# Gated conv blocks moved into the steps of the attention pipeline

## The chip, the cores and the metric

The kernel runs on one core of a Trainium2 chip. TensorE (PE) multiplies matrices, ScalarE (ACT) evaluates functions, VectorE (DVE) and GpSimd (POOL) work element by element, and SyncE (SP) starts the loads from DRAM. Each engine works through its own queue in order and waits where an operand is not ready. The metric is the device time of one execution in microseconds; less is better.

## The reference

Two layers of a diffusion backbone over 256 latent and 256 context tokens of width 1024, in float32. Each layer is a SwiGLU half step, a token mixing and a second SwiGLU half step. The change touches the mixing alone. It has three branches over the same normalised input, whose outputs are normalised, put side by side and projected (`merge_groups`):

```python
q_lat, kv_lat, k_pe, sg_in, cv_in = jnp.split(hn @ w_mix_in[l], splits, axis=-1)
q = mla_queries(q_lat, g_q_lat[l], w_q_up[l], g_q_head[l], rope)
k, v = mla_keys_values(kv_lat, k_pe, g_kv_lat[l], w_kv_up[l], g_k_head[l], rope)
attn = latent_attention(q, k, v, kc, vc)          # 8 heads, 96 wide keys, 64 wide values

def spatial_gating(sg_in, g_sgu, w_spatial, b_spatial):
    u, v = jnp.split(jax.nn.gelu(sg_in), 2, axis=-1)
    v = rms_norm(v.reshape(b, n, SG_GROUPS, SG_GROUP_DIM), g_sgu)
    ...
    return u * vs.reshape(b, n, SG_WIDTH)

def short_conv(cv_in, w_conv):
    b_gate, c_gate, xin = jnp.split(cv_in, 3, axis=-1)
    z = c_gate * xin
    y = lax.conv_general_dilated(z, ...)           # 3 taps, each channel by itself
    return b_gate * y
```

In the first layer (layer 0 below) latent and context tokens take all branches, 512 tokens. In the second (layer 1) the context gives keys and values only, so queries, gating and conv have 256 tokens.

## The kernel before

Weights come from DRAM in one stream, in the order of use. `Weights.pump` starts loads as room comes free and splits each weight in a high part (`whi`, ScalarE, L125) and a low part (`wlo`, L126, on GpSimd through the whole mixing, since `low` is "g" there). Each product is then three matmuls: high by high, high by low, low by high (`mm3`, L384 to L386, and `mm3x`, L389 to L391, with the operands' roles exchanged). At most five split weights are held. A weight `SPARE` in the stream is room lent to the attention. `W.hold` stops splitting except where `W.pump(n)` asks for it.

The schedule is written out by hand: jobs are emitted one after the other, and each engine's queue has its instructions in this order. PSUM has eight banks, six under the name `mm` and two under `sm`. A matmul into a bank waits until the bank's former readers are done.

The mixing of a layer (`mixing`, from L634) runs in this order:

- `kv_lat`, `kv_ctx`, `q_ctx` make key and query latents; `kv_tr` and `q_tr` transpose them (L720) and split them in two parts (L722, L723).
- `uv_lat` and `uv_ctx` project the gating's u and v; at their end `v_norm` normalises v for every tile of 128 tokens (L815 to L829: a square, a reduction, a root, four scalings, a split).
- `conv_block(0)` to `conv_block(3)`: 24 matmuls each. Of every three blocks the first gives the c gate, the second the product z and the three taps on VectorE (L872 to L877), the third the b gate's product (L879) and its squares.
- `spatial`: the gating's mixing over tokens, its product with u and its norm (L893 to L914).
- `conv_block(4)`, `conv_block(5)`, then `y_sg` (L921), which transposes the gating's result into the projection's input.
- `k_up` (L953): keys of four token tiles, each with a sum of squares, a root and an evacuation (L964 to L977). `y_cv_stats` takes the conv's norm, which is a root on ScalarE and a diagonal on VectorE.
- `q_up` (L1004): queries of each tile, whose rotary part is turned on GpSimd (L1037 to L1042).
- `y_cv`: the conv's norm is broadcast over TensorE and multiplied into the projection's input.
- `close_p1` gives the tiles of the first half back and opens those of the attention.
- `att(0)` to `att(11)`, the steps of a pipeline over heads. Step i takes `A(i)` (transposes of a head's queries and keys, L1076, each into an `sm` bank where there are four tiles), `B(i-2)` (scores, their maxima on VectorE, exponentials on ScalarE, the division by the sum on GpSimd, L1138), `C(i-3)` (transposes of the probabilities, L1158) and `Dv` (probabilities times values, L1181). The copies out of `A`'s banks (L1082 to L1087) are emitted in the step behind it; VectorE's share, `lows`, stands behind the maxima of `B`. Step 0 begins with `v_up`, the values of four tiles, whose evacuations are spread over steps 1 and 2. Steps 9 to 11 begin the output projection on the conv's and the gating's features.

In layer 0 `A` of a head fills both `sm` banks. ScalarE holds one set of functions at a time: `preload` puts a function of the next set ahead (Gelu before the u/v projection ends, Sqrt before `v_norm`, Exp at the end of `q_up`, Sqrt in step 10).

Of the kernel before, what the change touches and what calls it, by code (L numbers as in the profile page):

```python
# [39 lines left out]
# packed per-partition parameters: name -> columns for one layer  # L40
# [20 lines left out]
class Weights:  # L61
    """Streams weights in order: DRAM -> raw tile -> (high, low) float32r parts, ahead of their use.
    SPARE in the stream is room of one weight, left to other uses between its take and its done."""

    def __init__(self, nc, pool, raws):
# [18 lines left out]
        self.sub_fin = [False] * len(self.subs)  # L84
        self.sub_pref = 0
# [7 lines left out]
    def pump(self, preps=None):  # L93
        """Start the loads that have room, and prepare the parts (at most preps, when held back)."""
# [3 lines left out]
        while go:  # L98
# [8 lines left out]
            while left > 0 and self.prep_i < len(self.subs) and self.prep_i < self.sub_pref + SUBB:  # L107
# [67 lines left out]
def hybrid_trunk_kernel(ctx: ExitStack, tc: tile.TileContext, io: dict, out: bass.AP):  # L175
# [65 lines left out]
    # ---------------------------------------------------------------- weight specs  # L241
# [110 lines left out]
    def split_norm(src, dst_h, dst_l, rb, a, b=None, eng=None):  # L352
        """high and low parts of src * a * rb (+ b); returns the emission of the low part."""
# [17 lines left out]
    def staggered(makers):  # L371
        """runs emissions that return a follow-up, each follow-up one later"""
# [60 lines left out]
    # ---------------------------------------------------------------- FFN  # L433
    def ffn(l, which, ntok, tail, first=None):
        """tail(part): called by the last block to start the chain of what follows."""
# [28 lines left out]
        def first_two(W):  # L464
            """Blocks 0 and 1: the latent half while the norm of the context half is under way."""
# [147 lines left out]
    def boundary(l, i):  # L613
        """tail of the last block before norm i of layer l: work(0..2) is the ctx half in three parts."""
# [18 lines left out]
    # ---------------------------------------------------------------- mixing  # L633
    def mixing(l):  # L634
# [5 lines left out]
        def open_pools(W):  # L640
# [9 lines left out]
            st["row"] = per.tile([128, NROW], F32, name="row")  # L650
            SP.dma_start(out=st["row"], in_=io["row"][:, l])
            P["kvh"] = per.tile([128, 2, NTOK], F32R, name="kvh")
            P["kvl"] = per.tile([128, 2, NTOK], F32R, name="kvl")
# [9 lines left out]
            P["stok"] = P["guv"][:, :, 0:256]  # L663
            P["cvo"] = p1.tile([128, 2, NQ], F32, name="cvo")
# [948 lines left out]
```

## Time and profile before

| | |
|---|---|
| three runs, median | 1778.43 us (1777.52 to 1781.66) |
| the profiled execution, span | 1778.8 us |
| TensorE busy | 1715.4 us, 96% |
| VectorE, ScalarE, GpSimd busy | 1077.7, 661.1, 328.9 us |
| mean granted TensorE clock | 0.983 |

Times of the trace are microseconds from the start of the span. A matmul's recorded time is longer than the distance to the next one's start, since matmuls overlap in the array; the distance between starts is what a row of them costs. Square brackets behind an instruction give the idle time of its engine just before it and the instruction that ended the wait. `PEclk` is the granted clock of TensorE as a share of full speed.

### The profile page before, as it was taken

What the parts mean: (1) busy time and instruction counts of PE and PEld (TensorE: products, weight loads), DVE (VectorE), ACT (ScalarE), POOL (GpSimd) and SP (SyncE); (2) the same over time, 40 slices, a digit from 0 to 9 for tenths busy, and PEclk for the clock granted to TensorE, in tenths of its full rate; (3) what the DMA queues carried; (4) which work ended last, traced back from release to release, by engine and by line L of the source; (5) the groups of instructions that cost most, each with busy time, mean ns of one, the idle gap of its engine ahead of it and who ended that gap; (6) DMA issues with size and microseconds to landing.
All of it is one profiled execution on the core that took longest, in us unless ns stands there. A gap on an engine that the chain in (4) does not pass through costs nothing.

```text
span 1778.8 us, 24162 instructions
## 1 busy us (share of the span) xinstructions
PE 1715.4 (96%) x9422; PEld 1450.0 (82%) x9422; DVE 1077.7 (61%) x1778; ACT 661.1 (37%) x1124; POOL 328.9 (18%) x210
## 2 busy tenths in 40 slices
PE   8999999999998999999999999999999987889999
PEld 6888888889876688888888888888888986589999
DVE  5667777635578475575766356576765577554332
ACT  4422223224457443222232242222222355554442
POOL 0000000004346522000000030000000165465442
PEclk9999999999999999999999999999999998899999
DMA  8545555523211124454555234454454242136553
GB/s 318 189 158 181 184 182 191 178 84 98 82 60 48 37 70 151 134 176 155 165 175 166 98 107 158 162 164 161 158 174 123 70 142 69 36 116 210 185 180 94
DMA packets 71395, 248.59 MB, mean 140 GB/s; under 512 B 8048, under 2 KB 9584, under 8 KB 71280
## 3 DMA queue, kind: packets, MB, share of 16 engines
q1 hardware_dynamic: 71136, 246.97, 42.3%
q8 instruction: 74, 1.21, 0.3%
q14 instruction: 41, 0.34, 0.1%
q10 hardware_dynamic: 144, 0.07, 0.0%
HBM read 245.96 MB, written 1.05 MB: 139 GB/s over the span
## 4 chain that ended last, share of the span: by engine, by line
PE 87%; DVE 7%; ACT 3%; issue 2%; POOL 1%; DMA 1%; ACTq 0%; POOLq 0%; DVEq 0%
PE mm L384 26%; PE mm L385 25%; PE mm L386 25%; PE mm L389 2%; PE mm L391 2%; PE mm L390 2%; PE sm L288 1%; ACT p L1130 1%; PE sm L1181 1%; DVE mx L1119 1%; PE mm L1363 1%; DMA raw<-in_w_ada 1%; DVE xl L361 1%; PE sm L1076 1%; PE mm L1158 1%
## 5 line engine op out<-in xcount | busy, mean ns | idle before, releaser
L384 PE MATMUL mm<-xh,whi 128*128 128x512 f32 (+1 forms) x1712 | 612.0, 358 | 6.5 <-DVE kvl L723 3.1
L385 PE MATMUL mm<-xl,whi 128*128 128x512 f32 (+1 forms) x1712 | 605.7, 354 | 4.0 <-DVE xl L361 3.4
L386 PE MATMUL mm<-xh,wlo 128*128 128x512 f32 (+1 forms) x1712 | 604.1, 353 | 1.8 <-POOL wlo L126 1.3
L125 ACT ACTIVATE whi<-raw 128x1024 fp32r<-128x1024 f32 (+1 forms) x334 | 339.1, 1020 | 486.3 <-PE mm L385 373.6
L126 POOL TENSOR_TENSOR wlo<-raw,whi 128x1024 fp32r<-128x1024 f32 (+3 forms) x112 | 258.1, 2318 | 1335.7 <-ACT whi L125 1320.3
L126 DVE TENSOR_TENSOR wlo<-raw,whi 128x1024 fp32r<-128x1024 f32 (+2 forms) x222 | 265.9, 1199 | 244.8 <-ACT whi L125 244.8
L384 PEld LDWEIGHTS mm<-xh,whi 128*128 128x128 f32 x1712 | 327.4, 191 | 63.9 <-issue 11.8
L385 PEld LDWEIGHTS mm<-xl,whi 128*128 128x128 f32 x1712 | 327.4, 191 | 48.2 <-DVE xl L361 4.5
L386 PEld LDWEIGHTS mm<-xh,wlo 128*128 128x128 f32 x1712 | 327.4, 191 | 45.6 <-POOL wlo L126 1.5
L278 DVE SCALAR_TENSOR_TENSOR scratch<-raw,cs,scratch 128x512 f32<-128x512 f32 x448 | 307.4, 745 | 0.0
L384 PE MATMUL mm<-gh,whi 128*128 128x512 f32 (+1 forms) x770 | 270.2, 351 | 0.0
L386 PE MATMUL mm<-gh,wlo 128*128 128x512 f32 (+1 forms) x770 | 267.1, 347 | 0.0
L385 PE MATMUL mm<-gl,whi 128*128 128x512 f32 (+1 forms) x770 | 267.0, 347 | 0.0
L454 ACT ACTIVATE gh<-sa 128x512 fp32r<-128x512 f32 (+1 forms) x88 | 50.9, 579 | 310.2 <-DVE sa L453 310.2
L384 PEld LDWEIGHTS mm<-gh,whi 128*128 128x128 f32 x770 | 145.8, 189 | 22.3 <-issue 4.9
L386 PEld LDWEIGHTS mm<-gh,wlo 128*128 128x128 f32 x770 | 145.8, 189 | 18.3
L385 PEld LDWEIGHTS mm<-gl,whi 128*128 128x128 f32 x770 | 145.9, 189 | 17.5
L276 DVE TENSOR_SCALAR scratch<-raw,cs 128x512 f32<-128x512 f32 x64 | 28.2, 484 | 148.9 <-PE sm L288 148.9
L455 DVE TENSOR_TENSOR gl<-sa,gh 128x512 fp32r<-128x512 f32 (+1 forms) x88 | 57.7, 656 | 56.8 <-ACT gh L454 56.8
L453 DVE TENSOR_TENSOR sa<-sa,mm 128x512 f32<-128x512 f32 (+1 forms) x88 | 53.9, 613 | 17.7 <-PE mm L386 16.0
L408 DVE TENSOR_TENSOR acc<-acc,sq 128x256 f32<-128x256 f32 x63 | 41.4, 657 | 35.1 <-ACT sq L407 35.1
L360 ACT ACTIVATE xh<-scratch,mods 128x256 fp32r<-128x256 f32 x88 | 42.8, 506 | 52.9 <-DVE scratch L356 52.9
(207 smaller groups left out, 1457.6 us busy)
## 6 DMA issues: line engine op xcount, KB each, us to landing
raw<-in_w_ffn_in SPq DMA_DIRECT2D x176, 512.0 KB, 3.9
raw<-in_w_ada SPq DMA_DIRECT2D x144, 512.0 KB, 4.2
raw<-in_w_ffn_out SPq DMA_DIRECT2D x64, 512.0 KB, 4.4
raw<-in_w_ffn_out SPq DMA_DIRECT2D x32, 384.0 KB, 3.4
raw<-in_w_mo SPq DMA_DIRECT2D x16, 512.0 KB, 3.5
raw<-in_w_cv SPq DMA_DIRECT2D x12, 512.0 KB, 3.7
raw<-in_w_uv SPq DMA_DIRECT2D x8, 512.0 KB, 3.9
raw<-in_w_q SPq DMA_DIRECT2D x8, 384.0 KB, 3.1
```

Source lines behind the costliest of these rows:

```text
L125: nc.scalar.activation(hi[:, a:b], src, AF.Copy)
L126: eng.tensor_tensor(lo[:, a:b], src, hi[:, a:b].bitcast(F32), ALU.subtract)
L278: DVE.scalar_tensor_tensor(acc[:, s], src, cv, acc[:, s], ALU.mult, ALU.add)
L360: ACT.activation(dst_h, u, AF.Identity, bias=b)
L384: PE.matmul(bank, lhsT=wh, rhs=xh, start=first, stop=False)
L385: PE.matmul(bank, lhsT=wh, rhs=xl, start=False, stop=False)
L386: PE.matmul(bank, lhsT=wl, rhs=xh, start=False, stop=last)
L389: PE.matmul(bank, lhsT=xh, rhs=wh, start=first, stop=False)
L408: DVE.tensor_tensor(acc[:, half], acc[:, half], sq, ALU.add)
L453: DVE.tensor_tensor(sa[:, 0:n], sa[:, 0:n], bb[:, 0:n], ALU.mult)
L454: ACT.activation(st["gh"][:, m, 0:n], sa[:, 0:n], AF.Copy)
L455: DVE.tensor_tensor(st["gl"][:, m, 0:n], sa[:, 0:n], st["gh"][:, m, 0:n].bitcast(F32), ALU.subtract)
```

## The change

- The six conv blocks are no longer jobs of their own. `conv_block(W, i)` is called in attention step i, for i from 0 to 5, between `B` and `C`. `y_sg` is called in step 6, `y_cv_stats` and `y_cv` in step 8. The conv's tiles are taken from the attention's pool.
- Behind the u/v projection come `k_up`, `v_up`, `spatial`, `q_up` and `close_p1`. `v_up` evacuates each tile at once.
- `v_norm` of tile 0 stays at the end of the u/v projection; `v_norm` of tile t+1 is emitted inside `k_up`, behind tile t.
- In steps 0 and 1 the copies out of `A`'s banks follow at once.
- The gating's result stands in the scratch tile instead of in the queries' place. `kvh`, `kvl`, the row parameters and `pss` move to the pool of the first half.
- The stream has the weights in the new order (keys, values, gating, queries, spare, conv), one of them is split at the end of each of `k_up`, `v_up`, `spatial`, `q_up` and steps 0 to 6, and `Weights` counts the weights done instead of following the first one not done.
- Comments and docstrings are dropped.

The diff, cut to its core:

```diff
     def done(self, i):
-        self.sub_fin[i] = True
-        while self.sub_pref < len(self.subs) and self.sub_fin[self.sub_pref]:
-            self.sub_pref += 1
+        self.sub_done += 1
         self.pump()
...
-                v_norm((0, 1, 2, 3))
+                v_norm((0,))
             job(uv_ctx)
...
-        def conv_block(i):
+        def conv_block(W, i):
...
         def spatial(W):
             s, wh, wl = W.take()
+            P["stok"] = new_scratch()[:, 0:nq]
...
-        for i in range(6):
-            job(conv_block(i), [conv_spec[i // 2]] if i % 2 == 0 else [])
-            if i == 3:
-                job(spatial, sp_spec)
+            W.pump(1)
...
         def k_up(W):
...
                 last = fin
+                if t + 1 < nq:
+                    v_norm((t + 1,))
             last()
             W.done(s)
+            W.pump(1)
...
         def v_up(W):
...
-                def evac(t=t, bk=bk):
-                    if t % 2:
-                        DVE.tensor_copy(P["v"][:, t], bk)
-                    else:
-                        ACT.activation(P["v"][:, t], bk, AF.Copy)
-                evacs.append(evac)
+                if t % 2:
+                    DVE.tensor_copy(P["v"][:, t], bk)
+                else:
+                    ACT.activation(P["v"][:, t], bk, AF.Copy)
             W.done(s)
-            P["v_evac"] = evacs
+            W.pump(1)
...
-        job(y_sg)
         job(k_up, ku_spec)
-        job(y_cv_stats)
+        job(v_up, vu_spec)
+        job(spatial, sp_spec)
         job(q_up, qu_spec)
-        job(y_cv)
...
                 if i == H + 2:
                     preload(AF.Sqrt)
+                a = None
+                if i < 2:
+                    a = A(i)
+                    for f in a[0] + a[1]:
+                        f()
+                if i < 6:
+                    conv_block(W, i)
+                elif i == 6:
+                    y_sg(W)
+                elif i == 8:
+                    y_cv_stats(W)
                 late, evac = ([], []), []
                 if 0 <= i - 3 < H:
                     evac = C(i - 3)
...
-                if 1 < i < H - 1:
+                if i == 8:
+                    y_cv(W)
+                if i < H - 1:
                     W.pump(1)
...
         for i in range(H + 4):
-            job(att(i), vu_spec + [SPARE] if i == 0 else mo_spec(i - H - 1) if i > H else [])
+            cv = [] if i > 5 else conv_spec[i // 2][i % 2:i % 2 + 1]
+            job(att(i), ([SPARE] if i == 0 else []) + cv + (mo_spec(i - H - 1) if i > H else []))
```

## Rows read from the trace of the kernel before

**Rows 1.** The page's busy time of each engine, share of the span, instructions.

```profile
PE 1715.4 (96%) x9422; PEld 1450.0 (82%) x9422; DVE 1077.7 (61%) x1778; ACT 661.1 (37%) x1124; POOL 328.9 (18%) x210
```

**Rows 2.** Windows: stretch, length, busy time by engine (instructions), PEclk, DMA share, GB/s.

```profile
464.00:527.50 63.50, 61.89 (x304) 52.99 (x303) 47.54 (x108) 31.69 (x75) 26.14 (x23) 1.00 0.21 72
527.50:560.60 33.10, 24.80 (x148) 19.72 (x147) 25.25 (x46) 24.61 (x59) 18.21 (x18) 0.90 0.11 38
560.60:600.00 39.40, 37.23 (x247) 27.84 (x245) 22.52 (x50) 23.94 (x59) 21.53 (x26) 1.00 0.07 24
1442.60:1495.40 52.80, 42.38 (x266) 38.09 (x265) 44.31 (x85) 25.32 (x57) 29.48 (x23) 0.94 0.34 112
1495.40:1521.50 26.10, 20.34 (x101) 14.08 (x100) 16.90 (x33) 17.30 (x37) 17.41 (x13) 0.80 0.18 61
1521.50:1550.10 28.60, 24.88 (x163) 18.40 (x161) 14.19 (x30) 14.78 (x33) 10.74 (x12) 0.94 0.06 19
```

**Rows 3.** Waits of PE, 464 to 600: who waited for whom, total, times, longest.

```profile
PE sm L1076 <- DVE qTl L1083: 6.1, 4, 2.5
...
PE mm L389 <- DVE k_tok L975: 0.6, 1, 0.6
```

**Rows 4.** Waits of PE, 1442.6 to 1550.

```profile
PE mm L927 <- DVE q_tok L914: 5.7, 1, 5.7
PE mm L1158 <- POOL p L1138: 4.6, 7, 0.7
PE mm L384 <- DVE kvl L723: 3.1, 1, 3.1
```

**Rows 5.** Timeline of PE, conv: start, length, instruction.

```profile
464.56 0.48 PE L384 MATMUL mm<-xh,whi 128*128 128x512 f32 x1
...
486.45 0.28 PE L384 MATMUL mm<-vnh,whi 128*128 128x256 f32 x1
...
1464.98 0.28 PE L384 MATMUL mm<-xh,whi 128*128 128x256 f32 x1
1465.10 0.28 PE L385 MATMUL mm<-xl,whi 128*128 128x256 f32 x1
```

**Rows 6.** Timeline of DVE: two tiles of v_norm, then two of k_up.

```profile
471.58 0.41 DVE L821 TENSOR_REDUCE vss<-sa 128x4 f32<-128x256 f32 x1
...
474.39 0.41 DVE L821 TENSOR_REDUCE vss<-sa 128x4 f32<-128x256 f32 x1
...
509.35 0.69 DVE L975 TENSOR_TENSOR k_tok<-mm,hr 128x512 f32<-128x512 f32 x1
...
511.15 0.69 DVE L975 TENSOR_TENSOR k_tok<-mm,hr 128x512 f32<-128x512 f32 x1
```

**Rows 7.** Timelines of PE and POOL: end of q_up in both layers.

```profile
520.90 0.34 PE L391 MATMUL mm<-whi,qll 128*128 128x384 f32 x1
...
525.01 0.74 POOL L1042 TENSOR_TENSOR q_tok<-q_tok,row 128x256 f32<-128x256 f32 x1 [1.87 <-ACT q_tok L1024]
...
1488.10 0.34 PE L391 MATMUL mm<-whi,qll 128*128 128x384 f32 x1
...
1494.31 0.73 POOL L1040 TENSOR_TENSOR q_tok<-q_tok,qt 128x256 f32<-128x256 f32 x1
```

**Rows 8.** Timelines of PE and ACT, layer 0's last steps.

```profile
574.29 0.47 PE L389 MATMUL mm<-kTh,qTh 96*128 96x512 f32 x1
...
586.44 1.28 ACT L237 ACT_TABLE_LOAD   x1
...
588.08 1.47 PE L1158 MATMUL mm<-ident,p 128*128 128x128 f32 x12
```

**Rows 9.** Timelines of DVE and POOL: a tap of the conv, twice.

```profile
480.76 7.76 POOL L126 TENSOR_TENSOR wlo<-raw,whi 128x1024 fp32r<-128x1024 f32 x3 [15.13 <-ACT whi L125]
...
483.50 2.77 DVE L876 SCALAR_TENSOR_TENSOR vtmp<-z,vec,vtmp 128x512 f32<-128x512 f32 x1
...
499.42 0.75 DVE L876 SCALAR_TENSOR_TENSOR vtmp<-z,vec,vtmp 128x512 f32<-128x512 f32 x1
```

More of the change, by code (lines that the diff above doesn't have):

```diff
@@ L83, in __init__ @@
         self.sub_t = {}
-        self.sub_fin = [False] * len(self.subs)
-        self.sub_pref = 0
+        self.sub_done = 0
         self.prep_i = 0
@@ L106, in pump @@
                 go = True
-            while left > 0 and self.prep_i < len(self.subs) and self.prep_i < self.sub_pref + SUBB:
+            while left > 0 and self.prep_i < len(self.subs) and self.prep_i < self.sub_done + SUBB:
                 if self.subs[self.prep_i] is None:
@@ L649, in open_pools @@
             P["rqs"] = per.tile([128, nq, H], F32, name="rqs")
-            st["row"] = per.tile([128, NROW], F32, name="row")
+            st["row"] = p1.tile([128, NROW], F32, name="row")
             SP.dma_start(out=st["row"], in_=io["row"][:, l])
-            P["kvh"] = per.tile([128, 2, NTOK], F32R, name="kvh")
-            P["kvl"] = per.tile([128, 2, NTOK], F32R, name="kvl")
+            P["kvh"] = p1.tile([128, 2, NTOK], F32R, name="kvh")
+            P["kvl"] = p1.tile([128, 2, NTOK], F32R, name="kvl")
             P["qlh"] = p1.tile([128, 3, NQ], F32R, name="qlh")
@@ L790, in k_prep @@
             DVE.tensor_tensor(gqk, vcol(l, "gqn"), vcol(l, "gkn"), ALU.mult)
-            P["pss"] = per_t = P["per"].tile([128, 4], F32, name="pss")
+            P["pss"] = per_t = P["p1"].tile([128, 4], F32, name="pss")
             for t in range(4):
@@ L838, in uv_lat @@
                 preload(AF.Sqrt)
-                v_norm((0, 1))
+                v_norm((0,))
         job(uv_lat, uv_spec)
@@ L847, in uv_ctx @@
                 preload(AF.Sqrt)
[L848 removed]
+                v_norm((0,))
             job(uv_ctx)
[L852 removed]
+        def conv_block(W, i):
             blk, kind = divmod(i, 3)
[L855 to L887 removed]
@@ new lines, in conv_block @@
+            s, wh, wl = W.take()
+            bk = mm_bank()
+            sl = slice(0, NQ)
+            for k in range(DK):
+                mm3(bk[:, sl], wh[:, 128 * k:128 * k + 128], wl[:, 128 * k:128 * k + 128],
+                    st["xh"][:, k, sl], st["xl"][:, k, sl], k == 0, k == DK - 1)
+            W.done(s)
+            ns = NQ // 256
+            v3 = lambda a: a[:, sl].rearrange("p (s t) -> p s t", s=ns)
+            if kind == 0:
+                P["c_sb"] = temp(512, "sa", 2)
+                ACT.activation(P["c_sb"][:, sl], bk[:, sl], AF.Copy)
+            elif kind == 1:
+                z = P["z"]
+                DVE.tensor_tensor(z[:, 0:ns, 1:257], v3(P["c_sb"]), v3(bk), ALU.mult)
+                y = P["y"]
+                w3 = [vcol(l, "w_conv", 3 * blk + j) for j in range(3)]
+                DVE.tensor_scalar(v3(y), z[:, 0:ns, 0:256], w3[0], None, ALU.mult)
+                DVE.scalar_tensor_tensor(v3(y), z[:, 0:ns, 1:257], w3[1], v3(y), ALU.mult, ALU.add)
+                DVE.scalar_tensor_tensor(v3(y), z[:, 0:ns, 2:258], w3[2], v3(y), ALU.mult, ALU.add)
+            else:
+                DVE.tensor_tensor(P["cvo"][:, blk], P["y"][:, sl], bk[:, sl], ALU.mult)
+                if blk == 0:
+                    ACT.activation(P["cacc"][:, sl], P["cvo"][:, 0], AF.Square)
+                else:
+                    sq = temp(512, "sa", 2)
+                    ACT.activation(sq[:, sl], P["cvo"][:, 1], AF.Square)
+                    DVE.tensor_tensor(P["cacc"][:, sl], P["cacc"][:, sl], sq[:, sl], ALU.add)
@@ L1063, in close_p1 @@
             P["p2"] = P["es2"].enter_context(tc.tile_pool(name=f"pb{l}", bufs=1))
-            P["at"] = P["p2"].tile([128, 4, NQ], F32, name="at")
+            p2 = P["p2"]
+            P["at"] = p2.tile([128, 4, NQ], F32, name="at")
+            P["cvo"] = p2.tile([128, 2, NQ], F32, name="cvo")
+            P["cacc"] = p2.tile([128, NQ], F32, name="cacc")
+            P["y"] = p2.tile([128, NQ], F32, name="cy")
+            z = P["z"] = p2.tile([128, NQ // 256, 258], F32, name="z")
+            DVE.memset(z[:, :, 0:1], 0.0)
+            DVE.memset(z[:, :, 257:258], 0.0)
             new_acc()
@@ L1200, in fn @@
                 if i == 0:
-                    v_up(W)
                     P["spare"] = W.take()
@@ L1206, in fn @@
                     bk, ctx_part = B(i - 2, lows)
-                    if i == 2:
-                        for f in P.pop("v_evac")[2:4]:
-                            f()
                 else:
@@ L1219, in fn @@
                 if i >= 5 and (full or i % 2):
-                    a, b = Dv((i - 5) // 2, 0 if i % 2 else 2, bk if full and bk is not None else sm_bank())
-                    d_evac = [a]
-                    late[0].append(b)
+                    e, f = Dv((i - 5) // 2, 0 if i % 2 else 2, bk if full and bk is not None else sm_bank())
+                    d_evac = [e]
+                    late[0].append(f)
                 for f in evac + ctx_part[0:1] + d_evac + ctx_part[1:2]:
                     f()
-                if i < H:
+                if 2 <= i < H:
                     a = A(i)
-                    if i == 1:
-                        for f in a[0] + a[1]:
-                            f()
-                        for f in P["v_evac"][0:2]:
-                            f()
-                    else:
-                        late = (a[0] + late[0], a[1])
+                    late = (a[0] + late[0], a[1])
                 P["late"] = late
-                if 1 < i < H - 1:
+                if i == 8:
+                    y_cv(W)
+                if i < H - 1:
                     W.pump(1)
```

37 lines of the change are left out of this document (2 added, 35 removed).

## The prediction

> **What bounds the kernel now.** TensorE is busy 1715 of 1779 us [rows 1], so a change that issues the same matmuls can only move the time by what TensorE waits or by what it runs at the lower of its two clock levels (1.2 instead of 2.4 GHz). I read the windows by stage first, three in each layer [rows 2]: the front (from the end of the u/v projection to the first head's transposes), the first attention steps (0 to 5, until the fifth head's scores) and the last steps. Idle time is length less busy time. Layer 0: front 1.6, first steps 8.3, last steps 2.2. Layer 1: 10.4, 5.8, 3.7. The granted clock says what else goes: 0.90 over 33.1 us in layer 0's first steps is 3.3 us of pulses, 0.80 over 26.1 us in layer 1's is 5.2. Then the waits: in layer 0 the key and query transposes wait for VectorE to empty the two small PSUM banks [rows 3]; in layer 1 y_sg waits 5.7 us for the gating, a conv block 3.1 us for the key latents, and the probability transposes 4.6 us for GpSimd [rows 4]. So some 32 us of idle time and some 13 us of clock lie around the change. It spreads the conv's matmuls over the first steps, where they fill the waits, and takes the same cover off the front.
>
> **The work that moves.** A conv block is 24 matmuls. In layer 0 the 96 of blocks 0 to 3 run from 464.56 to 486.45, 0.228 us each, so 5.5 us a block and 32.8 for six; in layer 1 two starts stand 0.12 apart, so 2.9 a block, 17.3 for six [rows 5]. This is the same time in either place. y_sg, the conv's sums of squares and its broadcast (2.3 us of TensorE in layer 0, 1.5 in layer 1 by the same timeline) go to steps 6 and 8, also unchanged in themselves.
>
> **Front, layer 0: what was covered.** Before, v_norm of four token tiles ran on VectorE under conv blocks. One tile takes 2.81 us from one reduction to the next, waits for ScalarE included, and VectorE's queue is in order, so that is its price there [rows 6]. Now tile 0 stands ahead of k_up, and tiles 1 to 3 stand inside it, behind the reduction and scale of one key tile and the evacuation of the one before. A key tile takes 1.80 us of VectorE [rows 6]. From 471.6, where tile 0 is done, to the last key evacuation are 4 x 1.80 + 3 x 2.81 = 15.6, with two hand-overs to ScalarE some 16: 487.7. TensorE needs 1.2 (transposes) + 24 x 0.232 = 5.6 for the keys and has six banks: four keys and two value tiles fill them at 473. The third value tile must wait for key tile 0's evacuation (about 478), the fourth for tile 1's (482.6), the gating for tiles 2 and 3's (487.3 and 488.1); already now q_up waits for a key tile's readers in this way [rows 3]. q_up then starts at 488.8. Work until there is 13.9 us of the 25.5, so 11.6 us of waiting. Behind q_up, the first head's transposes need the last query tile's rotary part from GpSimd. It is done 4.8 us after the start of q_up's last matmul now, and v_up hid that [rows 7]; v_up has gone ahead. ScalarE will be less far behind then (it starts on tile 0 some 3 us after its matmuls, and needs 2.5 a tile against 3.2 of TensorE), so I take 3.4 of it. With the 1.6 of waits that fall away, **+13.4**. The gaps may drop the clock over the start of q_up (up to +3.6, so 17); if the queue is shorter than I make it, 8 is the other end.
>
> **First steps, layer 0.** Step i now holds the scores of head i-2 (2.1 us), a conv block (5.5), transposes. VectorE and ScalarE are busy 25.2 and 24.6 us in these six steps now [rows 2], some 32 and 28 with the conv's part, against 52 that TensorE will need, and the bank waits of rows 3 lie behind the conv's matmuls. The idle 8.3 and the clock's 3.3 go: **-11.6** (-8.3 if the clock stays low).
>
> **Last steps, layer 0.** y_sg fills a wait of step 6 (0.9 us of qTl). In step 8 the conv's norm comes between two heads' exponentials. A Sqrt there needs another function table than Exp, and each change is a load of 1.28 us on ScalarE [rows 8]: out and back. Its sums also need a small bank, which head 7's keys hold until VectorE has copied them, behind head 6's maxima. Today the time from head 6's scores to the last head's probability transposes is 13.8 us [rows 8], with TensorE nearly always busy between; I find some 3.7 us more, 2.3 of it moved work. **+1.4**, from -3 (step 6 and 7 gain, table loads hidden) to +5.
>
> **Layer 1.** Here the front has waits already. Conv block 1's wait for kvl becomes k_up's (3 us stays). With two tiles, v_norm tile 1 is the only one inside k_up; the third value tile still waits for key tile 0 (some 2 us), fourth tile and gating under 1 together. The 5.7 us in front of y_sg goes, but the first head now waits for q_tok: GpSimd ends 6.9 us after the start of q_up's last matmul now [rows 7], each of two tiles taking 2.4 us there, and the low part of a conv weight is queued ahead of them; I take 4.9. Sum of waits about 10.9 and some 3 of clock against 10.4 and 3.2: **+0.3** (-4 to +5). First steps: each of the other engines has some 17 us in the six steps [rows 2], 22 at most with the conv's part, against 33 of TensorE, so the 5.8 idle and most of the clock's 5.2 go, less 1 at the start behind q_tok's wait: **-10** (-5.8 to -11). Last steps: step 8 has no value product here, so the broadcast stands waiting for the norm some 3.5 us; the waits for GpSimd shrink by 3: **+0.5** (-2 to +4).
>
> **No cost.** kvh, kvl, row and pss change pools; conv weights are prepared one a step (ScalarE 1.0, GpSimd 2.4 us, both with room); the same number of weights stays ahead, counting instead of prefix only serves the held spare. The loads on SP have the same order but for the moved weights.
>
> **Sum:** 13.4 - 11.6 + 1.4 + 0.3 - 10 + 0.5 = -6.0 us. From the span of 1778.8 that is 1772.8; the runs' median lies 0.4 under the span, so 1772.4.
>
> **Rivals.**
> *Slower: the conv's taps hold VectorE in the steps.* The three tap products read SBUF alone. With GpSimd on a weight's low part they took 2.77 us, without it 0.75 [rows 9]. In steps 1 and 4 GpSimd has a weight and a head's probabilities to do. Steps 2 to 5 have some 5 us of VectorE each in layer 0 and 3 in layer 1 (rows 2, less the 5 and 4 of steps 0 and 1). If each tap waits, a block takes 7.8 us of VectorE, so step 4 in layer 0 needs 12.9 against 9.8 of TensorE (+3.1); in layer 1 a block takes 7.3, step 4 needs 10.5 against 5.7 (+4.8), and head 0's maxima stand behind block 1 (+5). That is +13: 1785.4. It decides once the taps lose over 6 us beyond the steps' slack. For it: rows 9. Against: one step of slack between scores and transposes. The Trainium skill, page "SBUF — State Buffer", section "Who interferes with whom", says that a VectorE instruction with two SBUF inputs and a GpSimd one that reads SBUF exclude each other for a whole instruction, in order of issue; the trace agrees in the 2.77, and by that rule each tap that meets a weight would lose a whole GpSimd instruction.
> *No change: step 8 is on the path.* If nothing absorbs the two loads, the norm and the products behind them, step 8 costs 2 x 1.28 + 2.4 in layer 0 and as much with a shorter queue, some 4, in layer 1, instead of my 1.9 in all: -6.0 + 7.1, 1779.5. For it: head 7's transposes are close behind their probabilities now. Against: mo products stand in steps 9 to 11. The Trainium skill, page "ScalarE: Activation LUTs", section "What ACT_TABLE_LOAD costs", gives 1.28 us and a drain of 1.38 for each change; rows 8 shows the 1.28, and four more loads at the page's whole figure would be an estimated 5.5 us above my sum's 1.28 each, 1778.
> *More gain: the front does not stall.* If key evacuations overtake (shorter hand-overs, clock held), layer 0's front costs 6 less and layer 1's 3 less: 1763.4. Against it: six banks and an in-order queue leave no way round.
> *It doesn't do what it says:* a conv block finds its weight not ready and the steps wait for GpSimd; at 1 us in twelve steps that is 1784.4. Against: a weight's 2.4 us per step of 5.7 at least.
>
> **Chances.** Forecast 0.47 (0.42 of it beyond 0.2%, which is about what a measurement can tell from no change), more gain 0.12, step 8 0.18 (0.16 within 0.2%), taps 0.18, weights 0.05. Faster 0.54, same 0.21, slower 0.25. The terms' ends don't all meet; 1763 to 1784 takes in more gain, step 8 and the near half of the slower cases.
>
> **What would show it.** Right: in layer 0, TensorE waits for k_tok's evacuation (L975 before) three times between k_up and q_up, 11 us together; the transposes' waits for qTl are gone until step 6; the granted clock is near 1.00 from conv block 1 to step 5 in both layers; q_tok's wait at the first transposes; a Sqrt and an Exp load in step 8. Wrong: taps of over 2 us followed by late maxima (taps); idle time of over 4 us in step 8 (step 8); no k_tok waits (more gain); waits for wlo in the steps (weights). The prediction fails if VectorE's 16 us between v_norm tile 0 and the last key evacuation are much off, since six banks pass every microsecond of it on to TensorE.

## The result: 11 us slower, and where

The changed kernel takes 1788.96 us (median of four runs, 1787.05 to 1790.04) against 1777.97 of the kernel before in the same comparison: a ratio of 1.0054, with a 95% interval of 1.0041 to 1.0068. The forecast was 1772.4, faster. The profiled execution after took 1788.09 and spans 1786.3. TensorE's busy time is what it was [rows 1], so the difference is waiting and clock:

```profile
PE 1716.3 (96%) x9422; PEld 1451.9 (81%) x9422; DVE 1067.2 (60%) x1774; ACT 665.8 (37%) x1128; POOL 328.9 (18%) x210
```

These are the six windows of after, the stages of [rows 2]: in each layer the front, the first steps and the last steps (stretch, its length, busy time of PE, PEld, DVE, ACT, POOL, granted clock, DMA share, GB/s).

```profile
462.42:504.80 42.38, 30.62 (x148) 26.69 (x146) 30.10 (x79) 23.16 (x60) 14.44 (x18) 0.88 0.17 52
504.80:558.80 54.00, 53.45 (x289) 45.10 (x290) 32.83 (x60) 29.49 (x62) 26.51 (x22) 0.97 0.17 60
558.80:610.76 51.96, 43.25 (x264) 31.64 (x261) 27.08 (x61) 30.45 (x69) 23.76 (x27) 0.93 0.06 21
1451.56:1485.97 34.41, 24.85 (x112) 19.79 (x110) 26.93 (x63) 19.94 (x46) 17.36 (x18) 0.88 0.31 107
1485.97:1520.23 34.26, 34.22 (x243) 31.44 (x244) 22.68 (x38) 17.97 (x37) 20.46 (x12) 0.92 0.28 93
1520.23:1557.22 36.99, 28.57 (x173) 22.13 (x170) 21.15 (x44) 21.52 (x45) 17.81 (x16) 0.86 0.08 29
```

Second and fifth row: in the first steps TensorE is now busy without a gap (53.45 of 54.00 us, 34.22 of 34.26). That is the gain that was hoped for. First and fourth: the fronts are short and idle for 12 and 10 us (the forecast's waits add up to 15.0 and 10.9). Third and sixth: in the last steps, where the kernel before idled 2.2 and 3.7 us, it now idles 8.7 and 8.4. Against the forecast, stage by stage (forecast: the length before, plus or less the work moved, plus the prediction's term; the border of layer 0's front is put at 505.35, the end of the wait for q_tok, as in layer 1, and not at the 504.80 of the first two rows):

| stage | before | forecast | after | off by |
|---|---|---|---|---|
| layer 0, front | 64.2 | 64.2 - 32.8 - 2.3 + 13.4 = 42.5 | 42.9 | +0.4 |
| first steps | 33.1 | 33.1 + 32.8 - 11.6 = 54.3 | 53.5 | -0.8 |
| last steps | 38.6 | 38.6 + 2.3 + 1.4 = 42.3 | 52.0 | **+9.7** |
| layer 1, front | 52.8 | 52.8 - 17.3 - 1.5 + 0.3 = 34.3 | 34.4 | +0.1 |
| first steps | 26.1 | 26.1 + 17.3 - 10 = 33.4 | 34.3 | +0.9 |
| last steps | 28.9 | 28.9 + 1.5 + 0.5 = 30.9 | 37.0 | **+6.1** |

The misses add up to 16.4 us, and 1772.4 + 16.4 = 1788.8. The close fit is in part chance: the spans of the two profiles are only 7.5 us apart, because 2.8 us outside the mixing layers, where nothing was edited, go the other way. Within the mixing layers nearly the whole error lies in the last steps. The waits of TensorE in layer 0 after (460 to 615; who waited for whom, total, times, longest):

```profile
PE mm L386 <- DVE k_tok L961: 7.0, 2, 5.3
PE mm L1174 <- ACT p L1123: 4.2, 2, 3.8
PE mm L381 <- DVE hr L958: 3.0, 1, 3.0
PE sm L1069 <- POOL q_tok L1028: 2.3, 1, 2.3
PE sm L329 <- DVE qTl L1076: 1.8, 1, 1.8
PE mm L1151 <- ACT p L1123: 1.6, 1, 1.6
```

and in layer 1 (1450 to 1560):

```profile
PE sm L346 <- DVE scratch L340: 5.6, 2, 4.2
PE mm L1069 <- POOL q_tok L1026: 4.5, 2, 2.4
PE mm L388 <- DVE kvl L718: 3.5, 1, 3.5
PE mm L1151 <- DVE qTl L1076: 2.2, 1, 2.2
```

k_tok, hr and q_tok are the front's waits (10.0 us for the banks in layer 0, 2.3 and 4.5 for GpSimd). The qTl waits of [rows 3] are gone from the first steps, and so is y_sg's of [rows 4]; the 4.6 us there for GpSimd's division are 1.4. New are the waits in the last steps: L1174, L329 and L1151 in layer 0; L346 (4.2 of its 5.6 us) and L1151 in layer 1. Steps 8 and 9 of layer 0 show what they are (timeline of after: start, length, engine, line, instruction, in brackets the idle time before it and what ended it; L386 are scores, L329 the conv norm's sums, L334 its root, L353 its products, L1112 maxima, L1174 the product with the values):

```profile
576.35 0.47 PE L386 MATMUL mm<-kTh,qTh 96*128 96x512 f32 x1
...
580.42 1.24 PE L329 MATMUL sm<-ones,cacc 128*128 128x1 f32 x8 [1.76 <-DVE qTl L1076]
580.64 1.28 ACT L334 ACT_TABLE_LOAD   x1
...
581.94 0.20 ACT L334 ACTIVATE st_m<-st_m 128x2 f32<-128x2 f32 x1
...
584.76 1.28 ACT L1123 ACT_TABLE_LOAD   x1
584.96 0.59 PE L386 MATMUL mm<-kTh,qTh 96*128 96x512 f32 x1
...
587.38 0.85 DVE L353 SCALAR_TENSOR_TENSOR scratch<-cvo,vec,sm 128x256 f32<-128x256 f32 x2
...
590.48 1.28 DVE L1112 TENSOR_REDUCE mx<-mm 128x1 f32<-128x512 f32 x2
...
593.15 0.43 PE L1174 MATMUL mm<-pt,v 128*64 128x256 f32 x1 [3.76 <-ACT p L1123]
...
599.52 1.47 PE L1151 MATMUL mm<-ident,p 128*128 128x128 f32 x12
```

and head 7's scores in the kernel before:

```profile
578.88 0.50 PE L389 MATMUL mm<-kTh,qTh 96*128 96x512 f32 x1
```

Head 6's scores start at 576.35. The sums wait 1.76 us for a small bank; ScalarE fetches the Sqrt table, the two roots pass, C(5)'s copies stand behind them, and head 6's second pair of exponentials waits for the table to come back (584.76). Head 7's scores are issued 8.6 us after head 6's; in the kernel before it was 4.6 (574.29 in [rows 8], and 578.88). Up to there TensorE waits only for the small bank; the other 2.1 us are the norm's own sums and broadcast. Then VectorE does the conv's products first, so head 7's maxima, whose scores are done at 587.4, start at 590.48, and the value product, whose bank they free through the exponentials, waits 3.76 us. From head 6's scores to the last head's transposes (599.52) are 23.2 us, against 13.8 in [rows 8]. Of these 9.4 us more, 5.3 are idle time and 2.1 the norm's matmuls; most of the rest is clock, which fell behind the wait of 3.76 us. Windows of that stretch before and after, and of after behind the wait:

```profile
574.29:588.08 13.79, 13.29 (x87) 10.17 (x85) 8.50 (x21) 10.91 (x28) 9.89 (x14) 1.00 0.01 2
576.35:599.52 23.17, 17.33 (x99) 12.61 (x97) 13.43 (x35) 15.72 (x36) 11.79 (x16) 0.93 0.00 1
593.15:599.52 6.37, 6.37 (x28) 4.11 (x29) 1.25 (x4) 4.68 (x11) 3.91 (x5) 0.73 0.00 0
```

A granted clock of 0.73 over 6.37 us costs 1.7 us. In layer 1 it is the broadcast that stands waiting, and behind its 4.21 us the granted clock is 0.52 from 1540.96 to 1546.20 (2.5 us):

```profile
1533.15 0.48 PE L386 MATMUL mm<-kTh,qTh 96*128 96x512 f32 x1
...
1538.17 1.28 ACT L334 ACT_TABLE_LOAD   x1
...
1540.96 1.19 PE L346 MATMUL sm<-scratch,ones 128*128 128x256 f32 x2 [4.21 <-DVE scratch L340]
1541.59 0.99 PE L386 MATMUL mm<-kTh,qTh 96*128 96x512 f32 x1
...
1545.73 1.28 ACT L1123 ACT_TABLE_LOAD   x1 [2.22 <-DVE nb L1108]
...
1551.03 0.98 PE L1151 MATMUL mm<-ident,p 128*128 128x128 f32 x7 [0.67 <-POOL p L1131]
```

### The profile page after: what moved, and what is told of

Read it like the earlier page. It is cut to its first block, busy times and chain, and to the rows that moved or that the text cites. A ratio compares the mean times of both kernels' runs of the same rounds, so it can differ in the third digit from the quotient of the medians.

```text
span 1786.3 us, 24140 instructions
## 1 busy us (share of the span) xinstructions
PE 1716.3 (96%) x9422; PEld 1451.9 (81%) x9422; DVE 1067.2 (60%) x1774; ACT 665.8 (37%) x1128; POOL 328.9 (18%) x210
## 4 chain that ended last, share of the span: by engine, by line
PE 85%; DVE 7%; ACT 3%; issue 2%; POOL 1%; DMA 1%; ACTq 0%; POOLq 0%; DVEq 0%
PE mm L381 26%; PE mm L382 25%; PE mm L383 25%; PE mm L388 2%; PE mm L386 2%; PE mm L387 2%; DVE xl L358 1%; PE sm L285 1%; ACT p L1123 1%; DMA raw<-in_w_ada 1%; DVE scratch L353 1%; DVE mx L1112 1%; PE sm L1069 1%; PE mm L1174 0%; POOL wlo L125 0%
## 5 line engine op out<-in xcount | busy, mean ns | idle before, releaser
L273 DVE TENSOR_SCALAR scratch<-raw,cs 128x512 f32<-128x512 f32 x64 | 28.3, 484 | 148.9 <-PE sm L285 148.9
```

## Experiments

Runs of one kernel spread over 1.5 to 10 us, and the granted clock over the span lies between 0.977 and 0.987. So beside the medians stand four distances in each layer, read from TensorE's timeline of each profile: from k_up's first matmul to head 0's scores (front and steps 0, 1), to head 4's (steps 2 to 5), to head 6's (6, 7), and to the attention's sums of squares (8 to 11). Each profile is one execution. Most distances repeat to about 0.1 us between kernels that share the code of a stretch, but not all: the first of layer 0 (54.1 to 54.5 or 55.5 to 55.7 for one and the same front), its third (16.9 or 17.6), the first of layer 1 (40.1 or 41.1) and its last (24.1 in after, 25.7 in e7). A difference of 1 us in one of these is no more than a hint. The first two distances of the kernel before hold other work and are left out.

| kernel | median | ratio to before, 95% | layer 0 | layer 1 |
|---|---|---|---|---|
| before | 1778.0 | | -, -, 13.6, 25.0 | -, -, 11.5, 17.3 |
| after | 1789.0 | 1.0041 to 1.0068 | 55.5, 39.6, 17.6, 34.4 | 41.1, 24.9, 12.9, 24.1 |
| e1_norm_late | 1780.9 | 0.9996 to 1.0015 | 54.2, 39.6, 16.9, 28.3 | 41.0, 24.9, 12.9, 20.0 |
| e2_no_table | 1787.3 | 1.0033 to 1.0058 | 54.1, 39.6, 16.9, 33.6 | 41.1, 24.9, 12.9, 22.7 |
| e3_cv_step9 | 1787.0 | 1.0037 to 1.0063 | 54.1, 39.6, 16.9, 32.3 | 40.1, 24.9, 12.9, 23.8 |
| e9_no_table_cv_step9 | 1783.4 | 1.0017 to 1.0039 | 55.7, 39.6, 16.9, 31.7 | 41.0, 24.9, 12.9, 21.1 |
| e4_norm_ysg_late | 1778.4 | 0.9994 to 1.0012 | 55.7, 39.6, 13.1, 30.3 | 41.0, 24.8, 13.8, 19.9 |
| e5_front | 1782.9 | 1.0002 to 1.0030 | 51.2, 39.6, 16.9, 32.8 | 38.4, 24.6, 14.3, 23.0 |
| e6_front_tail | 1774.0 | 0.9967 to 0.9988 | 51.2, 39.7, 13.1, 30.3 | 38.5, 24.7, 15.3, 19.9 |
| e7_layer1_only | 1778.1 | 0.9987 to 1.0008 | as before | 40.1, 24.9, 12.9, 25.7 |
| e8_layer0_only | 1790.4 | 1.0053 to 1.0087 | 54.5, 39.6, 17.6, 34.4 | as before |
| e10_front2_tail | 1778.7 | 0.9993 to 1.0012 | 49.7, 39.7, 13.1, 30.3 | 37.7, 25.4, 15.0, 19.8 |
| e11_front2_norm | 1779.4 | 0.9992 to 1.0010 | 49.7, 39.7, 18.2, 28.3 | 37.6, 25.5, 12.9, 20.0 |
| e12_placed | 1773.1 | 0.9955 to 0.9977 | 49.8, 39.6, 13.1, 30.3 | 37.7, 25.5, 15.4, 19.9 |
| e13_low_vector | 1787.7 | 1.0036 to 1.0062 | 53.5, 39.7, 16.9, 34.2 | 40.7, 24.9, 13.0, 24.0 |
| e14_placed_low_vector | 1768.3 | 0.9930 to 0.9958 | 49.7, 39.7, 13.1, 30.4 | 35.6, 24.8, 15.0, 19.9 |
| e15_front_tail_again | 1774.2 | 0.9960 to 0.9981 | 51.0, 39.6, 13.1, 30.4 | 38.3, 24.6, 15.3, 19.9 |

**The norm out of step 8 (e1).**

```
-                elif i == 8:
+                elif i == 10:
                     y_cv_stats(W)
-                if i == 8:
+                if i == 11:
                     y_cv(W)
...
-            mo_mm(P["mob"][j], P["mo"][j], SC, sl, True, False)
+            mo_mm(P["mob"][j], P["mo"][j], (4, 5), sl, True, False)
+            if j == 2:
+                for e in range(3):
+                    mo_mm(P["mob"][e], P["mo"][e], (6, 7), sl, False, False)
```

> The conv's norm is taken out of step 8: its sums and roots stand in step 10, behind the load of the Sqrt table that is there anyway, its products in step 11, and the output projection begins with blocks 4 and 5 alone. Theory 'norm' (the last steps were lost to step 8's norm, between the exponentials of heads 6 and 7): from the scores of head 6 to the last probability transposes 23.2 us become about 14.5 in layer 0 and 17.9 about 11.5 in layer 1, at most 1 us comes back in each layer in step 11, so about 12 us less than the changed kernel's 1789: 1777 (1775 to 1780), and 18 table loads instead of 22. Theory 'banks' (y_sg's two banks in step 6 delay all that follows): step 6 and what it passes on stay, 1786. Theory 'backlog' (the conv blocks leave VectorE and ScalarE late, and the tail is long whatever stands in it): within 3 us of 1789, the waits only under other names.

Measured: 1780.9, 8.1 less. In the profile the stretch from head 6's scores to the last probability transposes is 13.2 and 11.5 us (574.06 to 587.28, 1525.47 to 1536.95):

```profile
574.06 0.47 PE L386 MATMUL mm<-kTh,qTh 96*128 96x512 f32 x1
...
587.28 0.96 PE L1151 MATMUL mm<-ident,p 128*128 128x128 f32 x7
...
1525.47 0.48 PE L386 MATMUL mm<-kTh,qTh 96*128 96x512 f32 x1
...
1536.95 1.10 PE L1151 MATMUL mm<-ident,p 128*128 128x128 f32 x8
```

That is 10.0 and 6.4 less than in after, and in layer 0 no longer than before. Some comes back in steps 10 and 11, so the last stretch falls by 6.1 and 4.1 us, 10.2 in all (the profile is of e1's fastest run, so the 8.1 of the medians is the safer number); the granted clock over the last steps of layer 0 is 1.00 again (0.93 in after). "Norm" holds, though 1780.9 lies just above its range of 1775 to 1780; "banks" doesn't explain the bulk, and "backlog" falls. The edit also changes which output matmuls come first; that was not tried by itself. With this alone the change stands even with the kernel before.

**What in step 8 costs (e2, e3, e9).** e2 changes only the root's function (it leaves the square root out), e3 only the step of y_cv, e9 is both.

```
-            P["cdg"] = [stats(P["cacc"], s, 256) for s in halves()]
+            P["cdg"] = [stats(P["cacc"], s, 256, AF.Copy) for s in halves()]   # e2, e9
...
-                if i == 8:
+                if i == 9:                                                      # e3, e9
                     y_cv(W)
```

> Only the function of the conv norm's root is changed, from Sqrt to Copy, which needs no table load (so the square root of that norm is left out; every instruction keeps its place and shape). It prices the two loads of 1.28 us in each layer's step 8 alone. If both stand on the path in both layers: 4 x 1.28 = 5.1 us less than 1789, 1784. If the loss is VectorE's queue (the conv's norm ahead of head 7's maxima), the loads are mostly beside it: 0 to 2 us, 1787 to 1789.

> Only the conv norm's broadcast and products (y_cv) are emitted one step later, behind head 7's maxima and ahead of the output projection; the sums, roots and table loads stay in step 8. If VectorE's queue is what holds head 7 (3.2 us of it in layer 0, the broadcast's 4.2 us wait in layer 1): about 3 less in layer 0 and 4 in layer 1, 1782. If the table loads or the small bank's wait are: 1 to 2 us less, 1787 to 1788. If 'backlog': no change.

> Both single edits of step 8 at once: no table load (the conv norm's square root left out, every instruction kept) and the conv norm's products emitted in step 9 behind head 7's maxima. Alone they gave 1.7 and 2.0 us, the whole norm out of step 8 8.1. If the loads and VectorE's queue hold the same chain in turn (each hides the other), both together give nearly the whole: 1781 to 1783. If they add: 1785.3. If what is left is the sums themselves (their 1.8 us wait for the small bank, and ScalarE's copies behind the second root): 1784 to 1786 as well, and the time from head 6's scores to head 7's stays above 7 us.

Measured: 1.7, 2.0 and 5.5 us less. By the last stretch: the loads 0.8 in layer 0 and 1.4 in layer 1; the products' place 2.1 and 0.3; both 2.7 and 3.0, of the whole norm's 6.1 and 4.1. In layer 1 both together give more than the sum of the two, as if each covered the other; the medians say the same (5.5 against 3.7), but both differences are near the spread given above. In layer 0 they add, and 3.4 us stay with the norm's bare presence: in e9, with neither load nor products between them, head 7's scores still start 9.25 us after head 6's:

```profile
576.57 0.48 PE L386 MATMUL mm<-kTh,qTh 96*128 96x512 f32 x1
580.66 1.37 PE L329 MATMUL sm<-ones,cacc 128*128 128x1 f32 x8 [1.76 <-DVE qTl L1076]
...
585.82 0.50 PE L386 MATMUL mm<-kTh,qTh 96*128 96x512 f32 x1
```

and the window of e9 over C(5)'s transposes, which stand between the sums and the value product:

```profile
581.89:584.63 2.74, 2.74 (x14) 2.41 (x14) 2.32 (x6) 1.01 (x3) 1.54 (x2) 0.50 0.02 6
```

Of the 4.7 us more than before, TensorE waits 1.76 for the small bank, the sums take 1.2, and 1.3 are clock: at a granted clock of 0.50, the lower of the two levels, the transposes take 2.74 us instead of 1.44 in after. ScalarE waits 1.94 us for the second root's input with C(5)'s copies queued behind it, but no matmul before head 7's scores waits for ScalarE. Behind head 7 the output products wait 1.26 us for the norm's. The bank's wait and the clock were not separated. The table loads, which the forecast's rival put first, are 1.7 of 5.1 us.

**y_sg's banks (e4 against e1, e11 against e10).** y_sg moves from step 6 to the end of step 8, into small banks; the conv's norm late as in e1.

```
-                elif i == 6:
-                    y_sg(W)
...
+                if i == 8:
+                    y_sg(W)
...
-                bk = tr_bank()
+                bk = sm_bank()
```

> As the kernel with the conv norm in steps 10 and 11, and y_sg (the transposes of the gated features) also moved, from step 6 to the end of step 8, in the two small banks, which no head needs by then. Theory 'banks': step 6 falls from 10.5 us to some 7.5 in layer 0, 2 us less in layer 1, so about 4.5 us below the kernel that moves the norm alone: 1772.5. If step 6's waits are made good in steps 7 to 9 (they have the same VectorE and ScalarE work to wait for): within 1.5 us of it.

> As the kernel above, with y_sg back in step 6 in two of the six large banks. If y_sg's banks cost what the first pair showed (2.5 us): 2.5 above the kernel above. If that pair's difference was the clock of its runs: within 1 us of it.

Measured: 2.5 us less than e1 in the medians. By stages steps 6 and 7 of layer 0 fall by 3.8 us (16.9 to 13.1; C(3)'s wait of 1.6 us for a bank that head 4's exponentials held is gone), 2.0 come back in step 8, and layer 1 loses 0.8: 1.0 us in all. The second pair agrees: in layer 0 18.2 + 28.3 = 46.5 with y_sg in step 6 (e11) against 43.4 at the end of step 8 (e10), layer 1 the other way by 2.0; medians 0.7 apart, as the second expectation of e11 has it. So most of what y_sg costs in step 6 is made good elsewhere when it moves; what is left, some 1 us, is at the edge of what these runs resolve.

**The front (e5, e6, e15).** guv gets its own tile instead of lying in q_tok, the load of the Exp table goes behind the gating, and then:

```
         def k_up(W):
...
-                if t + 1 < nq:
-                    v_norm((t + 1,))
...
         def v_up(W):
...
+            v_norm((1,))
...
         def q_up(W):
...
+                if t + 2 < nq:
+                    v_norm((t + 2,))
...
-        job(spatial, sp_spec)
         job(q_up, qu_spec)
+        job(spatial, sp_spec)
```

> Only the front of the changed kernel is rearranged: the value norms (v_norm) of tiles 1 to 3 leave k_up, so that key banks are emptied first (tile 1 behind v_up, tiles 2 and 3 inside q_up, whose tiles are longer), and the spatial gating stands behind q_up, where its matmuls cover the wait for GpSimd's rotary part; for that u and v get a tile of their own. Theory 'front' (10 us of bank waits in layer 0's front, 3 in layer 1's, and 2.3 and 4.5 at the first transposes are the price of that order): layer 0's front falls by about 10, layer 1's by 4: 1789 becomes 1775 (1773 to 1779). Rival 'the queue is conserved' (VectorE has the same 16 us to do, q_up's reductions now wait behind v_norm and the first head's transposes behind the gating): 0 to 4 us less, 1785 to 1789.

> The rearranged front together with the conv norm in steps 10 and 11 and y_sg at the end of step 8. If front and last steps are separate losses, the gains add: the tail's 10.6 us below the changed kernel and the front's 14: about 1765, and then it is 12 us faster than the kernel before. If the first steps only pass on what the front saves (an earlier start runs into the same VectorE and weight preparation): 1772 to 1778.

> The kernel with the whole value norms and both fixes once more, on the same chip as the three above, so that they can be compared: 1774 if its earlier median holds.

Measured: e5 6.1 us less than after, between the two expectations; e6 4.3 less than e4 (1774.0; 1774.2 the second time): no full sum. By stages layer 0 gains 3.0 to 4.4 of its 10 us of bank waits, and layer 1 2.7, of which 1.4 go again in steps 6 and 7. The waits of e5's TensorE, 460 to 512, tell the rest:

```profile
PE mm L386 <- DVE k_tok L961: 2.5, 1, 2.5
PE sm L1069 <- POOL q_tok L1027: 2.3, 1, 2.3
PE mm L381 <- ACT vnh L822: 1.3, 1, 1.3
PE mm L383 <- POOL wlo L125: 1.2, 1, 1.2
```

The bank waits fell from 10.0 to 2.5, but the gating waits for the last value norm, the first transposes still for the rotary part, the first conv block for its weight, and that block ran at the lower clock (window of e5 over it, granted clock 0.69; 0.85 over the same block in after):

```profile
499.08:508.37 9.29, 8.07 (x27) 5.98 (x27) 3.85 (x13) 5.41 (x14) 4.77 (x2) 0.69 0.20 64
```

**One layer at a time (e7, e8).** The layers' code of before and after stand side by side; one layer takes each.

```
-    mixing(0)
+    mixing_before(0)      # e7; in e8 layer 1 instead
```

> Layer 0 has the order of the kernel before, layer 1 that of the changed one. By the stages of the two traces layer 1 costs 2.1 us less: 1776. If layer 1's gain came from what layer 0 left (the clock, the weights ahead): 1778 or more.

> Layer 0 has the order of the changed kernel, layer 1 that of the kernel before. By the stages layer 0 costs 12.4 us more, and 2.5 less fall between it and layer 1: 1788 if these 2.5 belong to layer 0's change, 1790.5 if not. With the kernel that changes layer 1 alone, the two differences from the kernel before should add up to the whole 11 us if the layers do not touch each other.

Measured: e7 1778.1 (ratio 0.9987 to 1.0008), e8 1790.4 (1.0053 to 1.0087). The differences from before, 0.0 and 12.3, add up to the change's 11 within the intervals: the layers don't touch each other, and the whole loss is layer 0's. Layer 1's 2 us of gain in the profile don't show in the times.

**GpSimd beside VectorE (e13), and the value norms cut up (e10, e12, e14).** e13 is after with the first conv block's weight prepared on VectorE. e10 is e6 with each value norm emitted in three pieces at successive points of v_up and q_up, and the spare weight taken at step 4, so that the first conv weight is prepared before q_up; e12 is e10 with its three small tiles in another pool; e14 is e12 with the edit of e13.

```
+            W.low = "v"                                # e13 (spatial), e14 (v_up)
             W.pump(1)
+            W.low = "g"
-            ssq, m, r = temp(4, "vs3", 3), temp(4, "vm3", 3), temp(4, "vr3", 3)   # e10: whole-program pool
+            ssq, m, r = mt(4, "vs3", 3), mt(4, "vm3", 3), mt(4, "vr3", 3)         # e12: closed before attention
```

> As the kernel with both fixes (1774.0), but each value norm is cut in three (sums; root and scaling; high and low part) that stand at successive points of v_up and q_up, so that ScalarE never waits for VectorE ahead of a query tile's copies, and the held spare weight is taken at step 4 instead of step 0, so that the first conv block's weight is prepared before q_up. In the kernel before this one the queue of ScalarE ended 5 us behind q_up's last matmul in layer 0, the gating waited 1.3, the first transposes 2.3 and 2.4, conv block 0 1.3 for its weight and ran at the lower clock (0.70 in its stretch). If these are the front's rest: 5 us less in layer 0 (3 of clock among them), 3 in layer 1: 1767 (1765 to 1770). If the clock stays low in step 0 and the attention steps run into VectorE earlier: 1771 to 1774.

> The changed kernel with one edit: the low part of the first conv block's weight (prepared behind the gating, while q_up runs) is made on VectorE (1.2 us) instead of GpSimd (2.4 us). In the changed kernel's trace the four scalings of the gated features, 1.25 us of VectorE by their cost in layer 1 (0.62 for two), took 3.34 while GpSimd made that part, ScalarE then waited 2.7 us for the first query tile's mean, and the first transposes 2.3 and 4.5 for GpSimd's rotary part. If this meeting of the two engines is what holds the query tiles: 1 to 2 us less in each layer's front, 1785 to 1787. If the queue of ScalarE is the limit: within 1 us of 1789.

> The kernel with the cut value norms and both fixes (1778.7), instruction for instruction the same; only its three small tiles (16 bytes a partition each, three buffers) move from the pool that lives through the whole program to the one that is closed before attention, so that every later tile has the addresses it has in the kernel before. In the profiles its mixing layers were 1.8 us shorter than those of the kernel with whole value norms (1774.0), but the output matmuls of the feed-forward layers, which no edit touches, took 399 instead of 394 ns each, and it lost some 2 us in each of three such stretches. If the placement does that: 1772. If it is a chance of those runs: 1778 to 1779.

> The placed kernel with the low part of the first conv block's weight on VectorE. In its twin's trace four scalings of the last value tile took 3.54 us instead of 0.87 beside GpSimd's 2.40 for that weight, ScalarE stood 3.5 us, and the first transposes waited 4.1. If that is the rest of the front: 2 to 3 us less than the placed kernel, 1769 to 1770. If the four query tiles' own 2.6 us each on ScalarE set the end: within 1 us of it.

Measured: e13 1.3 us less than after, with intervals that overlap. In after's timeline the gating's four scalings meet GpSimd's weight:

```profile
492.75 3.34 DVE L904 TENSOR_SCALAR scratch<-scratch,vrr 128x256 f32<-128x256 f32 x4
493.53 2.40 POOL L125 TENSOR_TENSOR wlo<-raw,whi 128x1024 fp32r<-128x1024 f32 x1 [4.20 <-ACT whi L124]
...
497.69 0.21 ACT L1014 ACTIVATE hm<-hm 128x8 f32<-128x8 f32 x1 [2.72 <-DVE hm L1013]
```

and in e13's:

```profile
492.61 1.14 DVE L904 TENSOR_SCALAR scratch<-scratch,vrr 128x256 f32<-128x256 f32 x4
...
493.67 1.22 DVE L125 TENSOR_TENSOR wlo<-raw,whi 128x1024 fp32r<-128x1024 f32 x1
...
496.05 0.21 ACT L1016 ACTIVATE hm<-hm 128x8 f32<-128x8 f32 x1 [1.21 <-DVE hm L1015]
```

The same four instructions take 1.14 us instead of 3.34, and ScalarE's wait falls by 1.5. The meeting is real, its price in the changed kernel small: 0.6 and 0.4 us by stages (0.6 against the kernels whose first distance is 54.1), since the query tiles' own queue on ScalarE stands next. The Trainium skill, page "SBUF — State Buffer", section "Who interferes with whom", says of a tensor_scalar in its two-port mode, too, that it and a GpSimd instruction shut each other out for a whole instruction; the two fences agree.

e10 was 4.6 us slower than e6, where 7 us less was expected, though its mixing layers are 1.8 us shorter. The loss lay in the feed-forward layers, which no edit touches: their output matmuls ran slower at full clock (groups by line and shape in e10, 310 to 400; the last number is the mean in ns):

```profile
L381 PE MATMUL mm<-gh,whi 128*128 128x512 f32 x114 | 45.5, 399 | 0.0
```

and in e12, the same instructions in the same order on each engine, with later tiles where the kernel before has them:

```profile
L381 PE MATMUL mm<-gh,whi 128*128 128x512 f32 x113 | 44.5, 394 | 0.0
```

e12 is 5.6 us faster than e10: 1773.1 (the kernel before had 1777.9 beside e10 and 1779.9 beside e12, so the session doesn't explain it). e14 is 4.8 faster again, 1768.3, 3.1 of it by stages, all in layer 1; in layer 0 the second head's transposes then wait for the first one's qTl (1.9 us). At 0.9944 of the kernel before it is the fastest of all: with front and last steps mended, and one weight prepared on VectorE, the change does bring 10 us.

## Why the prediction was wrong, step by step

**Right.** The fronts: 42.9 and 34.4 us against 42.5 and 34.3. The named mechanism came as told: VectorE's in-order queue of key tiles and value norms, passed on through six banks, 10.0 us of waits in layer 0 against 11.6, and at the places that were named (third value tile at 477.5 against 478, fourth at 482.2 against 482.6, q_up at 488.7 against 488.8; the mixing of after starts 0.9 us earlier); q_tok's waits 2.3 and 4.5 against 3.4 and 4.9. That the sum for layer 0 fits to 0.4 us is in part luck: the waits are 2.7 us shorter, and TensorE is busy 3.1 us longer than its work at full clock (30.6 us against 62.6 - 32.8 - 2.3 = 27.5), at a granted clock of 0.88. The prediction knew of that clock, up to +3.6, but left it out of its sum. One cause was missed inside them, GpSimd's weight beside VectorE, which by e13's stages is worth some half a microsecond a layer. The first steps: 53.5 and 34.3 against 54.3 and 33.4; the conv's matmuls fill every wait of [rows 3]. The taps were no bound: in layer 1 a tap took 2.40 us in step 1 and another 2.51 in step 4 beside GpSimd, as [rows 9] warned, but the step of slack swallowed them. No step waited for a weight.

**Wrong: the last steps.** The step that failed is the term "I find some 3.7 us more, 2.3 of it moved work. +1.4" and its twin "+0.5" of layer 1. Without the moved work the stages took 11.1 and 6.6 us more (52.0 - 38.6 - 2.3; 37.0 - 28.9 - 1.5), beyond the ends given, +5 and +4. The prediction saw the place, both table loads and the small bank's wait, and then set nearly all of it against "TensorE nearly always busy". That reads busy time as slack. The rows say the contrary: 13.3 of the 13.8 us from head 6's scores to head 7's transposes busy means that next to nothing is left there to cover a wait, and the next independent work (mo's products) stands behind head 7's value product in TensorE's own order. What it should have added is the chain that now joins two heads: sums behind qTl, root, diagonals, broadcast, products, each on another engine, with head 6's exponentials and head 7's maxima queued behind on two of them. The prediction's 3.7 us more measured 9.4 in that stretch. e1 shows that 8.1 us of the loss belong to this norm in the medians (10.2 by stages); e2, e3 and e9 that of the 8.1 the loads alone are 1.7, the products' place 2.0, both together 5.5. A part of it is clock, which the term had at nothing (1.7 and 2.5 us in the two layers of after). Of the last steps' miss of 15.8 us 5.6 lie outside what e1's stages give back, and most of that in steps 6 and 7, where the prediction put nothing: from head 4's scores to head 6's 17.6 and 12.9 us against 13.6 and 11.5 before, y_sg's own transposes (0.9 us in layer 0) among them. With y_sg in step 8 (e4) layer 0's steps 6 and 7 take 13.1, but 2.0 us come back in step 8; so its place is the cause of the longer steps, and only about 1 us of the total.

**The rival "step 8 is on the path"** had the right place and, with 5.0 + 4 = 9.0 us for the norm, the right size (8.1 in e1's medians, 10.2 by stages), but not its parts: it counted the durations of loads and norm, and without the loads only 1.7 us go, while waits of what queues behind, and the clock, make up the rest. No drain follows a load here: the one at 580.64 ends at 581.92, and ScalarE's next instruction starts at 581.94. Its sign, over 4 us of idle time, came in steps 8 and 9 of layer 0 (5.8 us in the stretch of 23.2) and in step 8 of layer 1 (4.2 in one wait). Its time, 1779.5, is short by the longer steps 6 and 7 and by what e1 doesn't give back. The range, 1763 to 1784, ended 5 us short: both terms of the last steps lie beyond the ends that they were given, by 6.1 and 2.6 us.

**The front's mending** shows the same from the other side: taking 7.5 us of bank waits away returned 3 to 4, since the next waits (gating, rotary part, first weight, low clock) lay close behind.

## What to carry to other kernels

A stage in which the bounding engine is busy throughout and whose chain passes several engines has no cover for a new dependent chain: price such a chain from its first wait to the last instruction queued behind it, not by its instructions, and look at the granted clock behind each new wait. Work without a chain (matmuls whose operands are ready) is what fits between pipeline steps; norms go where their function table is loaded anyway and other matmuls are queued behind them. When a kernel changes time outside the edited stage, compare the mean durations there before looking for a cause inside it.

## What the runs showed of the hardware

Three small tiles with three buffers of 16 bytes a partition each, placed ahead of others, went with untouched 512-column matmuls of 399 instead of 394 ns and a kernel 5.6 us slower (e10 against e12). Which address decides it was not tried. Four VectorE scalings with one SBUF tensor as input took 3.34 us beside one GpSimd instruction and 1.14 without it (after against e13); four with two such inputs 3.54 us in e10 and 0.88 when that weight was made on VectorE (e14).
